# One 512-column product for the rounded input and its residual in both FFNs' up-projections

## The chip, the core and the metric

The kernel runs on one core of a Trainium2 chip. The metric is the device time of one execution in microseconds (us). Engines are called PE (TensorE, matrix products), PEld (its loading of the stationary operand), DVE (VectorE), ACT (ScalarE), POOL (GpSimd) and SP (SyncE, which issues the transfers).

## What is computed

A decoder trunk of two layers on 256 tokens of width 2048. Each layer has a token mixer (forgetting attention in the first, sliding-window attention in the second) and then a gated FFN with a causal convolution of width 3. The change touches the FFN's up-projection, the first line here:

```python
def conv_ffn(h, w_up, conv_w, conv_b, w_down):
    u = h @ w_up                                   # (256, 2048) @ (2048, 11264)
    up = jnp.pad(u, ((0, 0), (CONV_WIDTH - 1, 0), (0, 0)))
    u = sum(up[:, j:j + S] * conv_w[j] for j in range(CONV_WIDTH)) + conv_b
    g, val = u[..., :D_FF], u[..., D_FF:]
    return (jax.nn.silu(g) * val) @ w_down         # D_FF = 5632
...
x = layer_norm(DEEPNORM_ALPHA * x + (1.0 + g2) * conv_ffn(x * (1 + sc2) + sh2, ...))
```

The vectors shift, scale and gate of all sub-layers come from `silu(c) @ ada_w[i] + ada_b[i]`, which is a product of one row with 2048 x 12288 weights for each layer.

## The kernel before, in words

**Three products for one.** Every large product is made of operands that are split in two: the value rounded to the matrix format (`h`, here `hH`; `wh`) and the residual (`hL`; `wl`). The product is then hH·wh + hL·wh + hH·wl, summed in one PSUM bank. A weight tile `w` holds 2 x 128 rows and 512 columns (512 KB). ACT rounds it to `wh` (line 266) and DVE subtracts to get `wl` (line 277); `wh` and `wl` have four buffers each (pool `hl`), `w` has ten.

**The up-projection.** `w_stationary` (line 328) makes one block of 512 columns of `u`, transposed: the weights are the stationary operand, and hH or hL, stored as 16 tiles of 128 x 256 (features x tokens), moves. `w_mm` (line 311) handles one weight tile: for each of its two row halves `i` and for each of four 128-column blocks `f` it issues three products of 256 columns, so 24 for a tile, 192 for a block of 512 columns (8 tiles). Four blocks share two PSUM banks, two in each, 256 columns wide. An FFN has 22 such blocks, 11 for the gate half and 11 for the value half, in turns, so both FFNs have 44 of them, 352 tiles and 8448 products. They run in two stages for each FFN (12 and 10 blocks), each followed by its part of the down-projection, in which `gT` (the gated result) is stationary and 512 columns of weights move.

**The evacuation.** After a block, `evac` (line 1063) is put into a list that is advanced one step at every weight tile (`run_post`, line 249). For each of the four blocks `f`, `conv` (line 1054) reads PSUM three times: ACT scales and adds the bias (line 1056, into the tile `u`), and two DVE operations add the shifted taps (lines 1057, 1059). The gate half then goes through Silu on ACT (line 1075). The value half is multiplied on DVE (line 1080) and split into `gT` by ACT and DVE (lines 84, 85). Two `yield`s per block spread the four blocks over eight weight tiles.

**Work in the background.** While the FFN runs, DVE also accumulates the ada products (line 395, `acc`), so many steps for each weight tile as a rate says (0.64 in the first FFN, 0.4 in the second), and at the start of each FFN the layer norm's affine part (lines 657 and 658, 24 pairs of 128 x 512 in the trace over three uses).

**What sets the order.** The kernel is written as a list of steps, and the framework's scheduler orders the instructions of each engine from it when the program is built; each engine then runs its list strictly in order. PSUM is one pool of eight banks, shared by products, transposes and the rest. At the start of an FFN the input is made in pieces: `modulate` (line 506) normalises and transposes 128-column pieces of x (line 484), and `mod_pair` (line 488) writes hH and hL.

Of the kernel before, what the change touches and what calls it, by code (L numbers as in the profile page):

```python
# [17 lines left out]
P = 128  # L18
D = 2048
S = 256  # L20
# [21 lines left out]
def hybrid_trunk(ctx: ExitStack, tc: tile.TileContext, a: dict, out: bass.AP):  # L42
# [25 lines left out]
    def w_banks():  # L68
        return [bank("ws").rearrange("p (a s) -> p a s", a=2) for _ in range(2)]
# [4 lines left out]
    def mm(o, lhsT, rhs, start=False, stop=False, **kw):  # L74
        return nc.tensor.matmul(o, lhsT, rhs, start=start, stop=stop, **kw)  # L75
# [11 lines left out]
    def split_v(h, l, src):  # L87
# [13 lines left out]
    nc.gpsimd.memset(ident, 0.0)  # L101
    nc.gpsimd.affine_select(out=ident, in_=ident, compare_op=ALU.not_equal, fill=1.0, base=0,
                            pattern=[[-1, P]], channel_multiplier=1)
    onep = cst.tile([P, P], F32, name="onep")
    nc.gpsimd.memset(onep, 1.0 / P)

    mask = cst.tile([P, 3, P], F32, name="mask")
    nc.gpsimd.memset(mask, 0.0)
# [10 lines left out]
                                    fill=1.0, base=-b, pattern=[[-1, FH]], channel_multiplier=1)  # L119

    x = cst.tile([P, NT, D], F32, name="x")
    csil = cst.tile([KC, P], F32, name="csil")
    nc.scalar.activation(csil, rows0[:KC, 0, :], AF.Silu)
    cact = cst.tile([P, KC], F32, name="cact")
    pt = bank()
# [47 lines left out]
    def rotary():  # L173

        nc.gpsimd.dma_start(sink, a["swa_sinks"][0].partition_broadcast(P))
        posr = cst.tile([NT, P], I32, name="posr")
# [3 lines left out]
        posf = cst.tile([NT, P], F32, name="posf")  # L180
        nc.vector.tensor_copy(posf, posr)
        yield
        pt = bank()
# [127 lines left out]
    def w_mm(ps, kc, h, l, last=KC - 1, first=0):  # L311

        for i in range(2):
            for f in range(4):
# [56 lines left out]
    def ada_vector(l, v):  # L371
# [26 lines left out]
        if row:  # L398
            while not ada["gate_free"]:
                yield  # L400
            ada["gate_free"] = False
            g = cst.tile([P, D], F32, tag="gate", name="gate")
            for j in range(D // 512):
                ps = bank()
                mm(ps, onep, acc[:, j * 512:(j + 1) * 512], start=True, stop=True)
                yield
                nc.scalar.activation(g[:, j * 512:(j + 1) * 512], ps, AF.Copy, bias=1.0)
            gates[l, v] = g
            return
        ps = []  # L410
# [638 lines left out]
    def conv_ffn(l):  # L1049
# [2 lines left out]
        cw = lambda j, f: ccol[:, l, j, f:f + 1]  # L1052

        def conv(pf, f):
            u = tp.tile([P, S], F32, tag="u", bufs=3, name="u")
            nc.scalar.activation(u, pf, AF.Identity, bias=cw(CW, f), scale=cw(2, f))  # L1056
            nc.vector.scalar_tensor_tensor(u[:, 1:], pf[:, :S - 1], cw(1, f), u[:, 1:],  # L1057
                                           op0=ALU.mult, op1=ALU.add)
            nc.vector.scalar_tensor_tensor(u[:, 2:], pf[:, :S - 2], cw(0, f), u[:, 2:],  # L1059
                                           op0=ALU.mult, op1=ALU.add)  # L1060
# [12 lines left out]
        def silu(sil):  # L1073
# [95 lines left out]
```

## Time and profile before

| | us |
|---|---|
| time, median of 3 runs (2255.63 to 2259.47) | 2257.53 |
| span of the profiled execution, first to last instruction | 2251.9 |
| PE busy | 2197.1 (98%) |
| PEld busy | 2017.8 (90%) |
| DVE busy | 1794.3 (80%) |
| ACT busy | 1175.0 (52%) |
| first FFN, up stages | 473 to 751 and 883 to 1107 |
| second FFN, up stages | 1498 to 1772 and 1905 to 2129 |

The page gives no time of its own for the profiled execution beside the span. The median of the runs is 5.6 us above that span: this is what lies around the first and the last instruction, and the prediction adds it to a span. In the rows of the trace, "a<-b,c" is the tile written and the tiles read; the first number of a row of the timeline is the start in us from the span's start, the second its length. Rows of one engine may overlap: an instruction's length holds a tail in which the next one already runs.

### The profile page before, as it was taken

Reading aid. Unit: us, or ns where it says so; the run is one execution under the profiler, and the core shown is the slowest. Engines: PE = TensorE matmul, PEld = TensorE weight load, DVE = VectorE, ACT = ScalarE, POOL = GpSimd, SP = SyncE. Lnnn points to the kernel's source line nnn. Section 1 sums busy time; section 2 is a strip of 40 time slices with the busy share of each in tenths; the row PEclk is TensorE's granted clock in tenths of the full one; section 3 lists DMA queues with packets and bytes.
Section 4 is the critical chain, followed back from the end, with each engine's and each line's share of the span. In section 5 each row is a group of like instructions: output and inputs, shape, how many; then the busy total and the mean of one; then the engine's idle time right before and its main releaser. Section 6 shows DMA issues by size and latency. Waiting matters only on the chain. (4 is left out here: it accounts for less than half of the span.)

```text
span 2251.9 us, 38292 instructions
## 1 busy us (share of the span) xinstructions
PE 2197.1 (98%) x14853; PEld 2017.8 (90%) x14853; DVE 1794.3 (80%) x2450; ACT 1175.0 (52%) x1897; POOL 22.8 (1%) x53
## 2 busy tenths in 40 slices
PE   6999999999999999999999999999999999999997
PEld 6999888889999888999987788889999888999986
DVE  6989999979978968788788989779787555666756
ACT  3445656555555443655634588755555533454532
POOL 0000000000000000000000000000000000000000
PEclk9999999999999999999999999999999999999999
DMA  9999999969979989789897767658887566666663
GB/s 339 381 360 365 361 345 323 329 202 339 324 240 310 322 285 337 249 302 309 265 313 282 256 231 251 215 162 303 264 265 257 177 193 194 188 188 189 190 193 112
DMA packets 274248, 602.99 MB, mean 268 GB/s; under 512 B 21063, under 2 KB 29961, under 8 KB 273553
## 3 DMA queue, kind: packets, MB, share of 16 engines
q1 hardware_dynamic: 273008, 595.85, 79.3%
q0 software_dynamic: 1056, 4.69, 0.6%
q8 instruction: 116, 1.90, 0.3%
q14 instruction: 68, 0.55, 0.1%
HBM read 598.37 MB, written 2.10 MB: 267 GB/s over the span
## 5 line engine op out<-in xcount | busy, mean ns | idle before, releaser
L266 ACT CAST wh<-w 128x1024 fp32r<-128x1024 f32 x728 | 764.1, 1051 | 836.0 <-PE ws L75 304.6
L277 DVE TENSOR_TENSOR wl<-w,wh 128x1024 fp32r<-128x1024 f32 x728 | 888.1, 1223 | 352.6 <-ACT wh L266 331.8
L75 PE MATMUL ws<-hH,wh 128*128 128x256 f32 x3328 | 935.2, 282 | 4.9 <-ACT hH L84 2.1
L75 PE MATMUL ws<-hH,wl 128*128 128x256 f32 x3328 | 929.7, 281 | 3.2 <-DVE wl L277 3.1
L75 PE MATMUL ws<-hL,wh 128*128 128x256 f32 x3328 | 931.2, 280 | 0.0
L75 PEld LDWEIGHTS ws<-hH,wh 128*128 128x128 f32 x3328 | 628.7, 189 | 9.4 <-ACT hH L84 2.3
L75 PEld LDWEIGHTS ws<-hL,wh 128*128 128x128 f32 x3328 | 629.9, 189 | 2.9 <-issue 1.9
L75 PEld LDWEIGHTS ws<-hH,wl 128*128 128x128 f32 x3328 | 628.0, 189 | 4.7 <-DVE wl L277 4.6
L75 PE MATMUL xs<-wh,gT 128*128 128x512 f32 x1408 | 435.9, 390 | 0.0
L75 PEld LDWEIGHTS xs<-wh,gT 128*128 128x128 f32 x1408 | 264.4, 188 | 54.8
L75 PE MATMUL xs<-wl,gT 128*128 128x512 f32 x704 | 274.1, 389 | 0.0
L395 DVE SCALAR_TENSOR_TENSOR acc<-wa,cact,acc 128x1024 f32<-128x1024 f32 x180 | 228.5, 1277 | 0.3 <-DMA wa<-in_ada_w_dram 0.3
L395 DVE SCALAR_TENSOR_TENSOR acc<-wa,cactp,acc 128x1024 f32<-128x1024 f32 x128 | 162.7, 1279 | 1.0 <-DMA acc<-in_ada_b_dram 1.0
L75 PEld LDWEIGHTS xs<-wl,gT 128*128 128x128 f32 x704 | 132.2, 188 | 27.0
L75 PE MATMUL xs<-wl,hH 128*128 128x512 f32 x352 | 141.0, 401 | 3.1 <-DVE wl L277 3.1
L75 PE MATMUL xs<-wh,hH 128*128 128x512 f32 x352 | 142.0, 409 | 0.3 <-ACT hH L494 0.3
L75 PE MATMUL xs<-wh,hL 128*128 128x512 f32 x352 | 138.7, 397 | 0.0
L1056 ACT ACTIVATE u<-ws,ccol 128x256 f32<-128x256 f32 x176 | 96.5, 561 | 57.6 <-PE ws L75 49.1
L75 PE MATMUL xs<-wh,oT 128*128 128x512 f32 x384 | 125.1, 395 | 0.1
L1057 DVE SCALAR_TENSOR_TENSOR u<-ws,ccol,u 128x255 f32<-128x255 f32 x176 | 82.9, 480 | 19.0 <-ACT u L1056 19.0
L75 PEld LDWEIGHTS xs<-wh,oT 128*128 128x128 f32 x384 | 72.1, 188 | 14.8 <-ACT oT L84 0.5
L1059 DVE SCALAR_TENSOR_TENSOR u<-ws,ccol,u 128x254 f32<-128x254 f32 x176 | 83.6, 480 | 2.1
(218 smaller groups left out, 1597.3 us busy)
## 6 DMA issues: line engine op xcount, KB each, us to landing
w<-in_ffn_w_up_dram SPq DMA_DIRECT2D x352, 512.0 KB, 4.6
wa<-in_ada_w_dram SPq DMA_DIRECT2D x320, 512.0 KB, 5.5
w<-in_ffn_w_down_dram SPq DMA_DIRECT2D x176, 512.0 KB, 5.0
w<-in_fox_w_in_dram SPq DMA_DIRECT2D x96, 512.0 KB, 7.2
wo<-in_ada_w_dram SPq DMA_DIRECT2D x48, 512.0 KB, 8.9
w<-in_swa_w_in_dram SPq DMA_DIRECT2D x40, 512.0 KB, 5.3
w<-in_fox_w_o_dram SPq DMA_DIRECT2D x32, 512.0 KB, 6.0
w<-in_swa_w_o_dram SPq DMA_DIRECT2D x32, 512.0 KB, 5.2
```

The source lines that it names most:

```text
L75: return nc.tensor.matmul(o, lhsT, rhs, start=start, stop=stop, **kw)
L266: pin(nc.scalar.copy(h, w), False)
L277: pin(nc.vector.tensor_tensor(l, w, f32(h), op=ALU.subtract), behind[0] > 0)
L395: pin(nc.vector.scalar_tensor_tensor(ac, wo, (cactp if row else cact)[:, k:k + 1], ac, op0=ALU.mult, op1=ALU.add), True)
L1056: nc.scalar.activation(u, pf, AF.Identity, bias=cw(CW, f), scale=cw(2, f))
L1057: nc.vector.scalar_tensor_tensor(u[:, 1:], pf[:, :S - 1], cw(1, f), u[:, 1:], op0=ALU.mult, op1=ALU.add)
L1059: nc.vector.scalar_tensor_tensor(u[:, 2:], pf[:, :S - 2], cw(0, f), u[:, 2:], op0=ALU.mult, op1=ALU.add)
```

## The change

hH and hL become the two halves of one tile, `hHL` (16 x 2 x 256), so that a piece of hH and the piece of hL lie side by side. A new `u_mm` issues, for each stationary block, one product of wh with 512 columns (hH and hL at once) and one of wl with the 256 columns of hH. The 512 columns fill a bank: its left half collects hH·wh + hH·wl, its right half hL·wh. So each of the four blocks gets a bank of its own (four banks for a block of 512 columns instead of two), and the loops are turned: `f` is the outer loop, the row half `i` the inner. In `conv` ACT copies the right half to SBUF (tile `c`), and DVE adds it to the left half in place in PSUM, before the three old operations. One of the two `yield`s for each block goes. The SBUF that `c` takes comes from three small tiles, which move into the ring of tile `t`, and from the constant `onep`, which goes (its factor 1/128 becomes a scale of the ACT operation behind it).

```diff
-    onep = cst.tile([P, P], F32, name="onep")
-    nc.gpsimd.memset(onep, 1.0 / P)
...
-    csil = cst.tile([KC, P], F32, name="csil")
+    csil = tp.tile([KC, P], F32, tag="t", name="csil")
...
+    def u_banks():
+        return [bank("us").rearrange("p (a s) -> p a s", a=2) for _ in range(4)]
+
+    def u_mm(ps, kc, h, l):
+
+        for f in range(4):
+            for i in range(2):
+                wh, wl = h[:, i, f * P:(f + 1) * P], l[:, i, f * P:(f + 1) * P]
+                mm(ps[f], wh, hHL[:, kc + i], start=kc + i == 0, skip_group_check=True)
+                mm(ps[f][:, 0, :], wl, hH[:, kc + i, :], stop=kc + i == KC - 1, skip_group_check=True)
...
     def w_stationary(wsrc, col):
-        ps = w_banks()
-        stream(wsrc, 0, col, list(range(KC)), lambda kc, h, l: w_mm(ps, kc, h, l))
+        ps = u_banks()
+        stream(wsrc, 0, col, list(range(KC)), lambda kc, h, l: u_mm(ps, kc, h, l))
...
-                mm(ps, onep, acc[:, j * 512:(j + 1) * 512], start=True, stop=True)
+                mm(ps, ones, acc[:, j * 512:(j + 1) * 512], start=True, stop=True)
...
-    hH = cst.tile([P, KC, S], F32R, name="hH")
-    hL = cst.tile([P, KC, S], F32R, name="hL")
+    hHL = cst.tile([P, KC, 2, S], F32R, name="hHL")
+    hH, hL = hHL[:, :, 0, :], hHL[:, :, 1, :]
...
         def conv(pf, f):
+            c = tp.tile([P, S], F32, tag="c", bufs=2, name="c")
+            nc.scalar.copy(c, pf[:, 1, :])
+            pf = pf[:, 0, :]
+            nc.vector.tensor_tensor(pf, pf, c, op=ALU.add)
             u = tp.tile([P, S], F32, tag="u", bufs=3, name="u")
...
             for f in range(5):
-                v = conv(ps[f // 2][:, f % 2, :], f0 + f) if f < 4 else None
+                v = conv(ps[f], f0 + f) if f < 4 else None
                 if u is not None:
                     then(f - 1, u)
                 u = v
                 yield
-                yield
```

The forgetting attention's own projections keep `w_mm` and its 256-column products. Three places show how the engines' lists move.

PE, in the middle of a weight tile of the first FFN's first block, before (two stationary blocks, three products each):

```order
L75 MATMUL ws<-hH,wh 128x256
L75 MATMUL ws<-hL,wh 128x256
L75 MATMUL ws<-hH,wl 128x256
L75 MATMUL ws<-hH,wh 128x256
L75 MATMUL ws<-hL,wh 128x256
L75 MATMUL ws<-hH,wl 128x256
```

and now, the same place (`us` are the new banks), where two stationary blocks take four products:

```order
L75 MATMUL us<-hHL,wh 128x512
L75 MATMUL us<-hHL,wl 128x256
L75 MATMUL us<-hHL,wh 128x512
L75 MATMUL us<-hHL,wl 128x256
L75 MATMUL us<-hHL,wh 128x512
```

Each pair of 256-column products with the same `wh` has become one of 512, and one load of `wh` has gone with it.

PE at the start of the first FFN, before (`sm<-ident,x` are the transposes of x; in brackets the engine whose signal is waited for):

```order
L484 MATMUL sm<-ident,x 128x128 [waits Activation_49]
L484 MATMUL sm<-ident,x 128x128 x3
L484 MATMUL sm<-ident,x 128x128 [waits DVE_49]
L484 MATMUL sm<-ident,x 128x128 x3
L75 MATMUL ws<-hH,wh 128x256 [waits Activation_49]
L75 MATMUL ws<-hH,wh 128x256
L484 MATMUL sm<-ident,x 128x128
L484 MATMUL sm<-ident,x 128x128 [waits DVE_49]
L484 MATMUL sm<-ident,x 128x128 x2
L484 MATMUL sm<-ident,x 128x128 [waits DVE_49]
```

and now:

```order
L493 MATMUL sm<-ident,x 128x128 [waits Activation_49]
L493 MATMUL sm<-ident,x 128x128 x3
L493 MATMUL sm<-ident,x 128x128 [waits DVE_49]
L493 MATMUL sm<-ident,x 128x128 x3
L75 MATMUL us<-hHL,wh 128x512 [waits DVE_49,Activation_49]
L75 MATMUL us<-hHL,wl 128x256
L75 MATMUL us<-hHL,wh 128x512 [waits DVE_49,Activation_49]
```

The first product now waits for DVE's hL as well, and eight transposes that stood between the first products stand behind the first weight tile.

DVE, in the evacuation of the first FFN's second block (a value half), before:

```order
L277 TENSOR_TENSOR wl<-w,wh 128x1024 [waits DMAHW1_49,PE_49]
L1057 SCALAR_TENSOR_TENSOR u<-ws,ccol,u 128x255
L1080 TENSOR_TENSOR u<-u,sil 128x256 [waits DVE_49]
L1059 SCALAR_TENSOR_TENSOR u<-ws,ccol,u 128x254 [waits DVE_49]
L277 TENSOR_TENSOR wl<-w,wh 128x1024 [waits DMAHW2_49,PE_49,Activation_49]
L85 TENSOR_TENSOR gT<-u,gT 128x256 [waits Activation_49]
L395 SCALAR_TENSOR_TENSOR acc<-wa,cactp,acc 128x1024 [waits DMAHW3_49]
L277 TENSOR_TENSOR wl<-w,wh 128x1024 [waits DMAHW4_49,PE_49]
```

and now, where the same block's evacuation begins:

```order
L1067 TENSOR_TENSOR us<-us,c 128x256 [waits Activation_49]
L275 TENSOR_TENSOR wl<-w,wh 128x1024 [waits DMAHW4_49,PE_49,Activation_49]
L1070 SCALAR_TENSOR_TENSOR u<-us,ccol,u 128x255 [waits Activation_49]
L1067 TENSOR_TENSOR us<-us,c 128x256
L1072 SCALAR_TENSOR_TENSOR u<-us,ccol,u 128x254 [waits DVE_49]
L404 SCALAR_TENSOR_TENSOR acc<-wa,cactp,acc 128x1024 [waits DMAHW3_49]
L1070 SCALAR_TENSOR_TENSOR u<-us,ccol,u 128x255 [waits Activation_49]
L1092 TENSOR_TENSOR u<-u,sil 128x256 [waits DVE_49]
L1072 SCALAR_TENSOR_TENSOR u<-us,ccol,u 128x254 [waits DVE_49]
L275 TENSOR_TENSOR wl<-w,wh 128x1024 [waits DMAHW5_49,PE_49]
```

Between two subtractions `wl` there stand seven other operations now where there were three, since a block is evacuated at every tile and not at every second one, and each brings an addition more.

More of the change, by code (lines that the diff above doesn't have):

```diff
@@ L175, in rotary @@
         nc.gpsimd.dma_start(sink, a["swa_sinks"][0].partition_broadcast(P))
-        posr = cst.tile([NT, P], I32, name="posr")
+        posr = tp.tile([NT, P], I32, tag="t", name="posr")
         nc.gpsimd.dma_start(posr, a["positions"].rearrange("b (t p) -> (b t) p", p=P))
@@ L179, in rotary @@
         nc.vector.tensor_scalar_mul(nsink, sink, -1.0)
-        posf = cst.tile([NT, P], F32, name="posf")
+        posf = tp.tile([NT, P], F32, tag="t", name="posf")
         nc.vector.tensor_copy(posf, posr)
@@ L404, in ada_vector @@
                 ps = bank()
-                mm(ps, onep, acc[:, j * 512:(j + 1) * 512], start=True, stop=True)
+                mm(ps, ones, acc[:, j * 512:(j + 1) * 512], start=True, stop=True)
                 yield
-                nc.scalar.activation(g[:, j * 512:(j + 1) * 512], ps, AF.Copy, bias=1.0)
+                nc.scalar.activation(g[:, j * 512:(j + 1) * 512], ps, AF.Copy, bias=1.0, scale=1.0 / P)
             gates[l, v] = g
```

## The prediction

> **What bounds the kernel now.** I read the page's first part, then the busy time by stretches of one block of 512 columns (22.4 us), and then the timeline of PE inside a stage.
>
> ```profile
> PE 2197.1 (98%) x14853; PEld 2017.8 (90%) x14853; DVE 1794.3 (80%) x2450; ACT 1175.0 (52%) x1897; POOL 22.8 (1%) x53
> ```
>
> PE is never idle for long. That alone does not say that PE is the bound in the stage that changes, so here are the stretches, four of the first FFN's first stage, two of its second, two of the second FFN's first stage and two of its last. The columns are the stretch, its length, then busy time and instructions of PE, PEld, DVE, ACT and POOL, granted clock, DMA share and GB/s.
>
> ```profile
> 505.40:527.80 22.40, 22.09 (x190) 21.88 (x189) 22.40 (x30) 12.39 (x16) 0.00 (x0) 1.00 0.93 308
> 527.80:550.20 22.40, 22.40 (x195) 22.40 (x194) 22.40 (x31) 11.96 (x16) 0.00 (x0) 1.00 0.99 365
> 550.20:572.60 22.40, 22.40 (x195) 22.40 (x194) 21.86 (x27) 12.73 (x18) 0.00 (x0) 1.00 0.99 355
> 572.60:595.00 22.40, 22.40 (x195) 22.40 (x194) 22.07 (x32) 12.07 (x17) 0.00 (x0) 1.00 0.94 323
> 1017.50:1039.90 22.40, 22.40 (x194) 22.40 (x193) 21.33 (x29) 11.93 (x17) 0.00 (x0) 1.00 0.89 290
> 1039.90:1062.30 22.40, 22.40 (x194) 22.40 (x193) 18.82 (x21) 11.76 (x17) 0.00 (x0) 1.00 0.93 325
> 1524.40:1546.80 22.40, 22.40 (x194) 22.40 (x194) 22.36 (x32) 12.77 (x17) 0.00 (x0) 1.00 0.88 296
> 1546.80:1569.20 22.40, 22.40 (x194) 22.40 (x194) 21.47 (x31) 12.12 (x18) 0.00 (x0) 1.00 0.95 332
> 2014.00:2036.40 22.40, 22.40 (x194) 22.40 (x194) 13.22 (x16) 11.68 (x16) 0.00 (x0) 1.00 0.65 187
> 2036.40:2058.80 22.40, 22.40 (x194) 22.40 (x194) 15.75 (x24) 11.85 (x16) 0.00 (x0) 1.00 0.68 190
> ```
>
> PE works through all of them, at full granted clock. DVE has a third of its time free in the last stage, some 10% in the first FFN's second stage, and nothing at the start of the first FFN. How far ahead of PE DVE is decides what more work on it costs:
>
> ```profile
> 522.19 1.23 DVE L277 TENSOR_TENSOR wl<-w,wh 128x1024 fp32r<-128x1024 f32 x1
> 523.48 0.39 PE L75 MATMUL ws<-hH,wl 128*128 128x256 f32 x1 [0.31 <-DVE wl L277]
> 2003.18 1.05 ACT L266 CAST wh<-w 128x1024 fp32r<-128x1024 f32 x1 [0.95 <-PE ws L75]
> 2007.06 1.23 DVE L277 TENSOR_TENSOR wl<-w,wh 128x1024 fp32r<-128x1024 f32 x1 [1.24 <-ACT wh L266]
> ```
>
> In the last stage DVE waits for ACT and ACT waits for PE to free one of four buffers: both are as far ahead as the buffers allow. At 523.48 the opposite holds: PE waits 0.31 us for a `wl` that ended at 523.42. So **PE is the bound in 43 of the 44 blocks, and DVE in the one around 520 us**.
>
> **The change, part by part.** First the products. Their pitch (start to start) decides, not their length, since they overlap.
>
> ```profile
> 2000.06 0.28 PE L75 MATMUL ws<-hL,wh 128*128 128x256 f32 x1
> 2011.96 0.28 PE L75 MATMUL ws<-hL,wh 128*128 128x256 f32 x1
> ...
> 1799.92 0.39 PE L75 MATMUL xs<-wl,gT 128*128 128x512 f32 x1
> 1811.48 0.39 PE L75 MATMUL xs<-wl,gT 128*128 128x512 f32 x1
> ...
> 1254.63 0.40 PE L75 MATMUL xs<-wh,hH 128*128 128x512 f32 x1
> 1257.43 0.40 PE L75 MATMUL xs<-wh,hH 128*128 128x512 f32 x1
> ```
>
> Between the first two rows lie 102 products of 256 columns: 11.90 / 102 = 116.7 ns each. Between the next two lie 51 of 512 columns in the down-projection: 11.56 / 51 = 226.7 ns. The last two, with 12 products between them, are of 512 columns as well, with hH as the stationary operand: 2.80 / 12 = 233.3 ns. The trace has no product with 512 columns of hH and hL moving. Its bounds are these two rows: at 233.3 it costs just what two products of 256 cost, and the gain is nothing; at 226.7 it saves 6.67 ns. No row of 512 columns is slower than two of 256, so a loss on PE is excluded as far as rows go. I take 226.7, since the stationary operand of the new product is a small streamed buffer, as gT is, and hH is not loaded. There are 8448 / 3 = 2816 such pairs: 2816 x 6.67 = **18.8 us less**. A further gain could lie in the product of `wl` that follows, whose load now hides behind 512 columns:
>
> ```profile
> 1100.47 0.60 PE L433 MATMUL sm<-ident,acc 128*128 128x128 f32 x4
> L433 PE MATMUL sm<-ident,acc 128*128 128x128 f32 x96 | 14.0, 274 | 1.4 <-DVE acc L395 1.4
> ```
>
> Transposes of 128 columns come at (0.60 - 0.274) / 3 = 109 ns, which no product with a load of its own undercuts here. If 256 columns came down to that, 2816 x (116.7 - 109) = 22 us more would go. I take none: the load of the next `wh` still has to hide behind those 256 columns, as now.
>
> Here the Trainium skill can be weighed, "TensorE: Matmul & The Clock Gate", section "Back-to-back issue gap": a warm product takes its columns over 2.4 GHz and 2.5 ns on top. By that only 2.5 ns go with each merged pair, an estimate of 2816 x 2.5 = 7.0 us in place of 18.8. The rows disagree with it in size (116.7 for 256 columns, where it gives 109), so I keep the rows.
>
> Second, the additions. Each of the 176 blocks of 128 columns gets one more DVE operation of 256 columns and one ACT copy.
>
> ```profile
> L616 DVE TENSOR_TENSOR x<-x,t 128x512 f32<-128x512 f32 x48 | 32.8, 684 | 0.2
> L614 DVE TENSOR_TENSOR t<-xs,gate 128x512 f32<-128x512 f32 x48 | 31.6, 684 | 12.5 <-PE xs L75 12.4
> 1999.98 0.42 DVE L85 TENSOR_TENSOR gT<-u,gT 128x256 fp32r<-128x256 f32 x1
> 2000.32 0.48 DVE L1059 SCALAR_TENSOR_TENSOR u<-ws,ccol,u 128x254 f32<-128x254 f32 x1
> 2000.71 0.42 DVE L85 TENSOR_TENSOR gT<-u,gT 128x256 fp32r<-128x256 f32 x1
> ```
>
> An operand in PSUM costs DVE nothing extra at 512 columns (684 ns both). The addition is new in writing PSUM. It cannot cost less than nothing, being added work; from above the tap operation bounds it, pitch 0.39; the plain 256-column operation has pitch 0.34, and I take that: 4 x 0.34 = 1.36 us more DVE per 512 columns. PE needs 22.4 - 64 x 0.00667 = 21.97 us for these now. The ACT copy is bounded by two rows:
>
> ```profile
> L712 ACT COPY pT<-T 128x384 f32<-128x384 f32 x48 | 22.7, 473 | 0.4
> L84 ACT CAST oT<-o 64x256 fp32r<-64x256 f32 x24 | 8.7, 363 | 4.8 <-PE o L75 4.4
> ```
>
> Four of them at 0.36 to 0.47 bring ACT from 12 to about 13.7 of 21.97 us: hidden by ACT's idle time. If ACT were full, 176 x 0.36 = 63 us would show.
>
> What the additions cost is read stage by stage. In the last stage DVE goes to 17.1 of 21.97: nothing. In the first FFN's second stage a value and a gate block take 21.33 + 18.82 + 2.72 = 42.9 of 43.9: nothing, with `wl` tiles waiting in four buffers to cover a value block's 22.7. In the first FFN's first stage the first three stretches quoted come to 22.40 + 22.40 + 21.86 + 4.08 = 70.7 us against 65.9 of PE, with no stock left at 523: 4.8 us too much, of which a part was DVE working ahead (it catches up by 570); I take **4 us**, at least 2, and with no stock at all some 4 more in later value blocks. In the second FFN two stretches come to 46.6 against 43.9, but PE has no wait for `wl` there now, so some stock is left: **1 us**. Evacuating a block at every tile instead of every second one brings this work earlier in the block and is in these numbers.
>
> Third, the start of each FFN.
>
> ```profile
> 473.01 0.54 PE L75 MATMUL ws<-hH,wh 128*128 128x256 f32 x2 [0.33 <-ACT hH L494]
> 473.35 1.91 PE L484 MATMUL sm<-ident,x 128*128 128x128 f32 x8
> 474.16 0.75 DVE L496 TENSOR_TENSOR hL<-t,hH 128x256 fp32r<-128x256 f32 x2
> 474.91 0.56 PE L75 MATMUL ws<-hL,wh 128*128 128x256 f32 x1
> ...
> 1500.05 0.56 PE L75 MATMUL ws<-hL,wh 128*128 128x256 f32 x1
> ```
>
> Now the first product needs both hL pieces (DVE, done at 474.91), and the eight transposes that PE did from 473.35 stand behind the first tile. PE is idle from 473.0 to 474.6 or a little later, **1.6 us**, and twice that for two FFNs: 3.2 us, bounded by half of it and, if the granted clock stays low longer, by 5 us each. DVE and ACT are ahead in this time, which is part of why I take 4 and not 4.8 above. The other edits (the layout of hHL, the scale in place of `onep`, the tiles in the ring of `t`) add no instruction; POOL loses one and SP's issues stay in number: nothing.
>
> **The sum** is -18.8 + 4 + 1 + 3.2 = -10.6 us on a span of 2251.9, so 2241.3. The medians of the runs lie 5.6 above the span: **2246.9 us**.
>
> **The rivals.** *512 columns cost what two times 256 cost.* Every pair with hH in it has the same rate in this trace, 233.3 for 512 and 116.7 for 256, and only gT and oT do better. Then nothing is gained and the 8.2 us stay: 2257.5 + 8.2 = **2265.7**, slower. It decides from a pitch of 226.7 + 6.67 - 8.2 / 2.816 = 230.4 ns upward. For it speaks that equality; against it that hH was loaded in that row and is streamed in the new one.
>
> *DVE becomes the bound in the first FFN.* The chain of a block now goes PE, ACT copy, DVE addition, ACT, DVE, DVE, and both engines run in order; an ACT queue that stands before a DVE addition stands before the next `wh` too. With half a microsecond of such gaps in each of 22 blocks DVE needs 22.0 on average and the first FFN loses its 9.4 us of gain: 2246.9 + 9.4 = **2256.3**, no change. Against it speaks the stock of `wl` in all blocks but the early ones.
>
> *Something in between:* a pitch of 230, the middle of both rows, gains 9.4 us, and the time is again **2256.3**. The skill's 2.5 ns per pair are near this, 2257.5 - 7.0 + 8.2 = 2258.7, an estimate.
>
> *The load hides better:* 256 columns at 109 ns too, 2246.9 - 22 = **2225**.
>
> **How the numbers follow.** The forecast has a chance of 0.40, equal cost 0.28, DVE as the bound 0.14, in between 0.10, the better load 0.08. A measurement of this kernel tells 0.2% (4.5 us) from no change. Of the forecast's 0.40, 0.35 are faster, 0.03 same, 0.02 slower (its costs could be 15 us instead of 8.2); of equal cost 0.25 slower and 0.03 same; of DVE as the bound 0.02, 0.05, 0.07; of in between 0.02, 0.04, 0.04; the better load is faster. Together faster 0.47, same 0.15, slower 0.38. The range from 2230 to 2268 leaves out most of the last case and the worst 0.1 of the slower ones; both signs being near, the likeliest case's own range is 2241 to 2254.
>
> **What would show it.** Right or wrong is read first from the pitch of two `us<-hHL,wh` rows with a `us<-hHL,wl` between: 343 ns for the forecast, 350 for the rival, in the last stage, where DVE is idle. Then from the last stage's length: 10 blocks in 219.7 us instead of 224. The cost shows as PE waiting for `wl` between 500 and 600 us, and as idle PE before the first `us` row. DVE's addition should have a pitch near 0.34. The prediction is wrong if PE waits for `wl` in the second stages, if the pitch is 350, or if ACT's `wh` waits for DVE's additions.

## The result, and the profile after

The changed kernel takes **2255.54 us** (median of 12 runs, 2253.07 to 2258.84), the kernel before 2257.41 in runs beside it (12 runs, 2255.23 to 2261.49). The ratio is 0.999, with a 95% interval from 0.9981 to 0.9998: 0.5 to 4.3 us less, where the forecast was 10.6 us less: about a fifth of it. The profiled execution has a span of 2254.8 us and a time of its own of 2256.56.

First the pitch, in the last stage. The two rows of 512 columns below have 32 other such rows between them, and a `wl` product behind each:

```profile
2000.08 0.39 PE L75 MATMUL us<-hHL,wh 128*128 128x512 f32 x1
2000.30 0.28 PE L75 MATMUL us<-hHL,wl 128*128 128x256 f32 x1
2000.42 0.39 PE L75 MATMUL us<-hHL,wh 128*128 128x512 f32 x1
...
2011.52 0.39 PE L75 MATMUL us<-hHL,wh 128*128 128x512 f32 x1
```

33 pairs take 11.44 us: **346.7 ns each**, where the triple before took 350.0 and the forecast was 343.3. Inside a pair the 512 columns take 228.5 ns and the 256 columns 118.2 (means of over 2700 steps each). The gain is 350.0 - 346.67 = 3.33 ns a pair: 2816 x 3.33 = 9.4 us.

Then the starts of the two FFNs, the first with the rows ahead of it:

```profile
473.07 1.12 PE L493 MATMUL sm<-ident,x 128*128 128x128 f32 x4 [2.43 <-ACT x L646]
...
474.58 1.11 PE L493 MATMUL sm<-ident,x 128*128 128x128 f32 x4 [0.40 <-DVE x L648]
...
476.72 0.75 DVE L505 TENSOR_TENSOR hHL<-t,hHL 128x256 fp32r<-128x256 f32 x2
...
477.28 0.77 PE L75 MATMUL us<-hHL,wh 128*128 128x512 f32 x1 [1.58 <-DVE hHL L505]
...
1504.72 0.76 PE L75 MATMUL us<-hHL,wh 128*128 128x512 f32 x1 [1.58 <-DVE hHL L505]
```

PE waits 1.58 us for DVE's hL, twice, as forecast. What the forecast left at nothing can be seen in the granted clock. These are stretches of 24 us around both starts, of the kernel before:

```profile
466.00:490.00 24.00, 20.39 (x149) 19.16 (x149) 21.27 (x38) 15.06 (x22) 1.12 (x2) 0.93 0.41 115
1490.00:1514.00 24.00, 20.48 (x147) 19.02 (x146) 21.27 (x37) 15.15 (x22) 1.11 (x2) 0.93 0.36 112
```

and of the changed kernel:

```profile
466.00:490.00 24.00, 19.59 (x91) 16.12 (x90) 18.18 (x33) 12.04 (x18) 1.12 (x2) 0.79 0.31 104
1490.00:1514.00 24.00, 19.60 (x85) 15.86 (x85) 16.83 (x30) 11.58 (x16) 1.11 (x2) 0.79 0.26 93
```

The clock (the column ahead of the DMA share) falls from 0.93 to 0.79. At half clock (stretches of 1 us from 474 and from 481 us show 0.50) that is 0.07 x 24 / 0.5 = 3.4 us before and 10.1 us after. The Trainium skill, "TensorE: Matmul & The Clock Gate", section "What's actually happening", has the clock decided in windows of about 3.4 us; the stretches here (3.4, 6.7 and 10.1 in the runs below) are steps of that size.

That the wait lengthens the half clock is not shown, though. The kernel before, profiled once more, and the version without the additions (a run below), whose PE waits for hL as the changed kernel's does, lie closer together:

```profile
466.00:490.00 24.00, 20.39 (x121) 17.92 (x120) 18.02 (x33) 13.31 (x19) 1.12 (x2) 0.93 0.29 100
1490.00:1514.00 24.00, 21.16 (x105) 17.87 (x104) 16.73 (x30) 12.39 (x17) 1.11 (x2) 0.86 0.31 99
```

```profile
466.00:490.00 24.00, 19.14 (x95) 15.86 (x94) 18.59 (x33) 12.74 (x19) 1.12 (x2) 0.86 0.33 109
1490.00:1514.00 24.00, 18.69 (x95) 15.60 (x94) 18.96 (x34) 12.68 (x19) 1.11 (x2) 0.86 0.33 107
```

Nor does the mean clock of the executions follow the wait: it is 0.9888 for the kernel before and 0.9889 with the start mended, neither of which has the wait, and 0.9894 without the additions, which has it.

Third, DVE in the early first FFN, and what the additions are. The first fence holds PE's waits between 476 and 756 us, the next a row of the timeline, the third groups of the page:

```profile
PE us L75 <- DVE wl L275: 3.2, 3, 1.6
PE us L75 <- DVE hHL L505: 1.6, 1, 1.6
```

```profile
523.96 1.22 DVE L275 TENSOR_TENSOR wl<-w,wh 128x1024 fp32r<-128x1024 f32 x1
...
525.23 0.38 PE L75 MATMUL us<-hHL,wl 128*128 128x256 f32 x1 [1.64 <-DVE wl L275]
```

```profile
L1067 DVE TENSOR_TENSOR us<-us,c 128x256 f32<-128x256 f32 x176 | 71.1, 424 | 0.0
L1065 ACT COPY c<-us 128x256 f32<-128x256 f32 x176 | 61.6, 372 | 9.5 <-PE us L75 7.3
L1069 ACT ACTIVATE u<-us,ccol 128x256 f32<-128x256 f32 x176 | 98.1, 562 | 39.4 <-DVE us L1067 39.4
```

PE waits three times for `wl`, 3.2 us together against 0.3 us before. After 570 us there is no such wait in either FFN. ACT does wait 39.4 us for the additions, but that is idle time of an engine that is no bound.

Stage by stage, in us from the first product of one stage to the first of the next (the start is from the last product of the projection ahead):

| stage | before | after | start mended | no addition | two of 256 | mixed | slower early ada |
|---|---|---|---|---|---|---|---|
| up to the first FFN | 467.7 | 470.2 | 472.6 | 470.6 | 469.9 | 468.7 | 469.4 |
| start, first FFN | 5.3 | 7.0 | 5.5 | 7.0 | 5.5 | 5.5 | 5.5 |
| first FFN, first up stage | 277.5 | 279.6 | 277.8 | 276.1 | 281.3 | 277.0 | 275.6 |
| first FFN, second up stage | 227.0 | 224.9 | 224.9 | 224.9 | 227.0 | 224.9 | 224.9 |
| start, second FFN | 5.3 | 7.0 | 5.5 | 7.0 | 5.3 | 5.3 | 5.5 |
| second FFN, first up stage | 276.6 | 275.3 | 274.9 | 275.0 | 276.5 | 274.5 | 275.2 |
| second FFN, last up stage | 224.0 | 221.9 | 221.9 | 221.9 | 224.0 | 221.9 | 221.9 |

The second stages gain 2.1 us, which is 640 x 3.33 ns. The starts lose 1.7 each. The first up stages should have gained 2.6 us each (12 blocks): the second FFN's gains 1.3, the first FFN's loses 2.0. The first line differs by 2.5 us, though hardly anything was changed there; a run below takes that up. (In the kernel before the second and third up stage end at 1110 and 1775 us, not at the 1107 and 1772 given above.)

### The profile page after: what moved, and what is told of

It is laid out like the page before. It is cut to its first block, busy times and chain, and to the rows that moved or that the text cites. A ratio compares the mean times of both kernels' runs of the same rounds, so it can differ in the third digit from the quotient of the medians.

```text
span 2254.8 us, 33096 instructions
## 1 busy us (share of the span) xinstructions
PE 2196.5 (97%) x12037; PEld 1901.8 (84%) x12037; DVE 1847.4 (82%) x2626; ACT 1220.7 (54%) x2073; POOL 22.6 (1%) x52
## 5 line engine op out<-in xcount | busy, mean ns | idle before, releaser
L75 PE MATMUL us<-hHL,wh 128*128 128x512 f32 x2816 | 985.7, 393 | 3.2 <-DVE hHL L505 3.2
L75 PE MATMUL us<-hHL,wl 128*128 128x256 f32 x2816 | 792.0, 283 | 3.2 <-DVE wl L275 3.2
L75 PEld LDWEIGHTS us<-hHL,wh 128*128 128x128 f32 x2816 | 530.2, 188 | 115.8 <-ACT hHL L503 3.9
L75 PEld LDWEIGHTS us<-hHL,wl 128*128 128x128 f32 x2816 | 534.4, 190 | 8.0 <-DVE wl L275 4.6
L75 PE MATMUL xs<-wh,hHL 128*128 128x512 f32 x704 | 238.5, 404 | 0.3 <-ACT wh L264 0.2
L75 PE MATMUL ws<-hHL,wh 128*128 128x256 f32 x1024 | 190.1, 288 | 4.4 <-ACT hHL L84 2.1
L75 PEld LDWEIGHTS ws<-hHL,wh 128*128 128x128 f32 x1024 | 162.0, 195 | 7.4 <-ACT hHL L84 2.7
L75 PEld LDWEIGHTS xs<-wh,hHL 128*128 128x128 f32 x704 | 131.8, 190 | 30.0 <-issue 1.0
L75 PE MATMUL ws<-hHL,wl 128*128 128x256 f32 x512 | 143.7, 288 | 2.2 <-DVE wl L275 2.2
L75 PE MATMUL xs<-wl,hHL 128*128 128x512 f32 x352 | 141.7, 403 | 1.5 <-DVE wl L275 1.4
L1069 ACT ACTIVATE u<-us,ccol 128x256 f32<-128x256 f32 x176 | 98.1, 562 | 39.4 <-DVE us L1067 39.4
```

## The experiments

Times are put as ratios to the kernel before, in runs on the same chip (medians there 2258.2 to 2260.0 us); the changed kernel itself stands at 0.999. The 95% intervals reach some 0.001 to either side, so a difference of 2 or 3 us between two versions lies at the edge of the noise, and the stages of the table must bear it out.

**The start mended.**

```diff
+        if kc < nfirst[0]:
+            for i in range(2):
+                for f in range(4):
...
+                    mm(ps[f][:, 0, :], wh, hH[:, kc + i, :], start=kc + i == 0, skip_group_check=True)
+                    mm(ps[f][:, 0, :], wl, hH[:, kc + i, :], skip_group_check=True)
+            for i in range(2):
+                for f in range(4):
+                    mm(ps[f][:, 1, :], h[:, i, f * P:(f + 1) * P], hL[:, kc + i, :], skip_group_check=True)
+            return
```

> The first weight tile of each FFN is done in 256-column products, the 16 that need only hH first and the 8 with hL last; all else is the changed kernel (2255.5 us). Theory A (the product pair is 346.7 ns and not 343.3, gain 9.4 us, and the starts and the early stall of DVE give it back): PE's wait of 2.0 us before the first product goes, the half-clock stretch of 10.2 us at each FFN's start falls back to 3.4, and the time falls by 2 to 3 us for the second FFN and by 0 to 3 for the first, where DVE becomes late next: about 2251. Rival B (the starts lie beside DVE's backlog and cost nothing; the gain is lost in the additions alone): 2255.5, and the waits for wl near 520 us grow by what the start gives.

0.9978 (0.9969 to 0.9987), 2253.39 us: 2.7 us below the changed kernel by the ratios. PE goes from the transposes straight into the products, and the clock of the same stretch is 0.86:

```profile
476.94 1.11 PE L505 MATMUL sm<-ident,x 128*128 128x128 f32 x4 [0.39 <-DVE x L660]
478.07 0.58 PE L75 MATMUL us<-hHL,wh 128*128 128x256 f32 x1
```

```profile
466.00:490.00 24.00, 20.94 (x108) 17.49 (x107) 17.94 (x33) 13.07 (x19) 1.12 (x2) 0.86 0.33 107
```

Theory A holds in size, at the low end of its 2 to 6 us: the two rows of the starts give back 1.5 us each. Rival B falls: the waits for `wl` did not grow but fell to 1.7 us. The half clock did not fall to 3.4 us as expected; it stays at 6.7 us, as long as in the version without the additions, which still has the wait.

**No addition.**

```diff
-            c = tp.tile([P, S], F32, tag="c", bufs=2, name="c")
-            nc.scalar.copy(c, pf[:, 1, :])
             pf = pf[:, 0, :]
-            nc.vector.tensor_tensor(pf, pf, c, op=ALU.add)
```

> The changed kernel without ACT's copy and DVE's addition: the right half of each bank is computed and never read, so the contribution of hL times wh is left out of the result. Theory A: only the early first FFN was short of DVE time, so the gaps before wl products at 523, 530 and 553 us (4.2 us together) go and the time falls by 4 to 5 us, to about 2251; the product pair stays at 346.7 ns. Rival B (the additions cost all of the missing gain, by writing PSUM while PE accumulates there): the pair falls to 343 ns and the time by 10 us or more, to 2245 or less.

0.9975 (0.9964 to 0.9985), 2252.69 us: 3.4 below the changed kernel. The first FFN's first stage takes 276.1 in place of 279.6; every other stage is within 0.4 of the changed kernel, and the pair stays at 346.7. So ACT's copies and DVE's additions cost 3.4 us, all in that stage. Rival B falls with the pair.

**Two of 256.**

```diff
-                mm(ps[f], wh, hHL[:, kc + i], start=kc + i == 0, skip_group_check=True)
+                mm(ps[f][:, 0, :], wh, hH[:, kc + i, :], start=kc + i == 0, skip_group_check=True)
+                mm(ps[f][:, 1, :], wh, hL[:, kc + i, :], skip_group_check=True)
```

> The changed kernel with each 512-column product made as two of 256 columns into the two halves of the same bank; banks, loop order, copy and addition stay. Theory A: the triple is 350.0 ns against 346.7, so the last stage takes 223.9 us instead of 221.8 and the time rises by 9.4 us, to about 2265. Rival of equal cost (the 512-column product gains nothing and the shorter stages come from the order of the loops or the banks): no change, 2255.5. Forecast as predicted (18.8 us in the products, lost elsewhere): 2274.

1.0014 (1.0005 to 1.0023), 2261.85 us: 5.4 above the changed kernel, not 9.4. The stages say why: the products cost their 9.4 us again (the two second stages are back at 227.0 and 224.0), but the first product waits for hH alone again, so both starts fell back to 5.5 and 5.3, 3.2 us together. The expectation had left that out. The last stage is 224.0 as before: banks and loop order do nothing to the pitch.

**The second `yield` restored** in `evac`.

> The changed kernel with the second yield of each evacuation step restored, so that a block's additions are spread over eight weight tiles again and its four banks stay in use longer. Theory A: the early first FFN lacks DVE time in sum, not in order, so 2255.5 within 1.5 us, and the gaps before wl products only move. Rival C (the bunched evacuation is what holds up the wl subtractions): the gaps at 523 to 554 us shrink below 1 us together and the time falls by 3 to 4 us. Rival D: banks are freed too late, PE waits for a bank at the start of a block, some us slower.

0.9991 (0.998 to 1.0001), 2256.03 us: as theory A has it, no change. PE's waits for `wl` become one of 1.8 us in place of three of 3.2 us together; the stage is 279.1.

**Mixed.** The first six blocks of the first FFN and the first two of the second are made the old way.

```diff
+                old = b < (3, 1)[l]
-                ps = w_stationary(w_up, b * WB)
+                ps = w_stationary(w_up, b * WB, old)
```

> The first six blocks of the first FFN and the first two of the second are made as in the kernel before (256-column products, two banks, two yields, no copy, no addition); the other 36 blocks as in the changed kernel. Theory A (the stages' difference to the kernel before is made of 0.21 us gained in every block, 1.7 us and about 1.2 us of half clock lost at each start, and about 3.6 us lost to DVE before 570 us): both losses go, 36 x 0.21 = 7.6 us stay, so 7 to 8 us below the kernel before and about 5.5 below the changed kernel; no PE wait for wl over 0.5 us anywhere in the FFNs. Rival B (the additions cost time in every block): the first FFN's second stage and the second FFN's stages are not shorter than in the changed kernel, and the whole gains less than 4 us on the kernel before.

0.9962 (0.995 to 0.9975), 2249.63 us: 8.6 us below the kernel before, a little over the 7 to 8 expected. PE's wait for `wl` is 0.3 us, as before. With both losses gone the gain of the products is what remains, so rival B (a cost in every block) falls.

**Slower early ada**, on top of the mended start.

```diff
             for b in range(b0, b1):
+                if l == 0 and si == 0:
+                    then(lambda b=b: ada.update(rate=0.4 if b < 2 else 0.76))
```

> The changed kernel with the first weight tile of each FFN done in 256-column products as in the run on the start, and with the ada accumulation slowed in the first four blocks of the first FFN (0.4 steps for each weight tile in place of 0.64) and made up in the other eight blocks of that stage (0.76). All 44 blocks but the first tiles keep the 512-column product and the additions. Theory A (early DVE is short by the sum of its work, and has room later): the gaps before wl products near 523 to 553 us shrink to under 1 us together, the first FFN's first stage takes about 275 us (277.8 in the run on the start), and the whole is 7 to 9 us below the kernel before, equal to the mixed kernel within a microsecond or two. Rival E (DVE has no room later either): the waits come back between 570 and 750 us and the stage stays at 277 us or more.

0.9959 (0.9945 to 0.9972), 2248.49 us: the fastest version, 9.3 us below the kernel before. PE waits for no `wl` in the first FFN's first stage, which takes 275.6 us, 2.1 less than with the mended start alone. DVE's early shortage was the sum of its work in some 100 us, and the additions fit in once other work makes room.

Those six runs settle the bookkeeping. The rest asks why the pair takes 346.7 ns and not 343.3.

**Grouped:** the eight products of 512 columns of a tile first, then the eight of 256.

```diff
         for f in range(4):
             for i in range(2):
-                mm(ps[f], wh, hHL[:, kc + i], start=kc + i == 0, skip_group_check=True)
-                mm(ps[f][:, 0, :], wl, hH[:, kc + i, :], stop=kc + i == KC - 1, skip_group_check=True)
+                mm(ps[f], h[:, i, f * P:(f + 1) * P], hHL[:, kc + i], start=kc + i == 0, skip_group_check=True)
+        for f in range(4):
+            for i in range(2):
+                mm(ps[f][:, 0, :], l[:, i, f * P:(f + 1) * P], hH[:, kc + i, :], stop=kc + i == KC - 1,
+                   skip_group_check=True)
```

> The changed kernel with the products of a weight tile in another order: the eight of 512 columns first, then the eight of 256. Theory P (a change of length between two products in a row costs time, since the next load hides behind a shorter product): 14 of 16 steps are between equals, 512 columns come at 226.7 ns and 256 at 116.7, the pair at 343.5 in the mean, the last stage at about 219.9 us instead of 221.8, and the whole some 8 us faster than the changed kernel. Theory Q (512 columns of hH and hL moving cost 228.5 and 256 of hH behind a load of wl cost 118.2, whatever stands beside): 346.7 and no change in the last stage. The wl products come later in a tile, so the early waits for wl may shrink by about 1 us in both cases.

1.003 (1.0018 to 1.0042), 2266.16 us. Neither theory had this. Rows of the last stage, eight products in the second and in the third:

```profile
2001.62 2.03 PE L75 MATMUL us<-hHL,wh 128*128 128x512 f32 x8
2003.48 1.11 PE L75 MATMUL us<-hHL,wl 128*128 128x256 f32 x8
2004.42 0.86 PE L75 MATMUL us<-hHL,wh 128*128 128x512 f32 x3
```

1.86 / 8 = 232.5 and 0.94 / 8 = 117.5 ns: the equal cost of the prediction's first rival, and the last stage takes 224.5 us. The mixture of lengths does not cost the missing half. In this layout it is what brings the gain.

**All of 512 columns.**

```diff
-                mm(ps[f][:, 0, :], wl, hH[:, kc + i, :], stop=kc + i == KC - 1, skip_group_check=True)
+                mm(ps[f], wl, hHL[:, kc + i], stop=kc + i == KC - 1, skip_group_check=True)
```

> The product of wl takes 512 columns too (hH and hL moving), which adds the term hL times wl to the result; every product of the up-projection then has 512 columns. Theory P (the mix of lengths costs): all at 226.7 ns as in the down-projection, 453.3 for two, the last stage of ten blocks at 640 x 0.4533 = 290.1 us. Theory Q (it is the moving tile): about 228.5 each, 457 for two, 292.5 us. Rival H (hH as an operand of 512 columns costs what it costs as stationary operand in the attention projections): 233.3 each, 298.7 us.

2589.24 us. Rival H holds: the rows below are 20 products apart, 4.67 / 20 = 233.5 ns, and the last stage takes 298.7 us.

```profile
2000.23 0.39 PE L75 MATMUL us<-hHL,wh 128*128 128x512 f32 x1
...
2004.90 0.39 PE L75 MATMUL us<-hHL,wh 128*128 128x512 f32 x1
```

**Zeros** in hH and hL (`nc.vector.memset(G, 0.0)` and the same for `B`, ahead of `modulate`).

> The changed kernel with scale and shift of the inputs of the sliding-window projections and of both FFNs set to zero, so that hH, hL and all that is made of them hold zeros; instructions, shapes and places stay, two small DVE operations more at each start. Theory Z (the pitch depends on the values that go through PE): 512 columns with hH stationary in the attention projections fall from 233.3 to about 226.7 ns, and the pair in the FFN from 346.7 to 343 or less (the last stage to 219.7 us or less). Theory Y (it does not): 233.3, 346.7 and 221.8 us again.

2255.89 us. Two rows with 33 pairs between them:

```profile
2020.23 0.39 PE L75 MATMUL us<-hHL,wh 128*128 128x512 f32 x1
...
2031.67 0.39 PE L75 MATMUL us<-hHL,wh 128*128 128x512 f32 x1
```

11.44 / 33 = 346.7 ns again, and 233.1 in the attention projections: theory Y. The values of hH and hL play no part.

**Shifted by 32 bytes:** a small tile ahead of hHL moves it and all that lies behind it.

> A tile of 32 bytes is placed ahead of hHL, so that hHL begins at 32 modulo 64 bytes in SBUF and the weights, wh, wl and gT at 0, the other way round than in the changed kernel. Theory S (the place of the operands in a 64-byte row sets the pitch): 512 columns of hHL fall to 226.7 ns and the down-projection's products, with wh and wl moving, rise from 226.7 to 228 or more. Theory Q (it does not): 228.5 and 118.2 in the up-projection, 226.7 in the down-projection, as before.

2253.03 us. All pitches as in the changed kernel, so theory S falls. hHL and the weights stay 32 bytes apart modulo 128 here, so the shift moved them together. What it left untried was their distance.

**Another place for gT.**

```diff
+    gp = ctx.enter_context(tc.tile_pool(name="gp", bufs=30))
     cst = ctx.enter_context(tc.tile_pool(name="cst", bufs=1))
...
-    gp = ctx.enter_context(tc.tile_pool(name="gp", bufs=30))
```

> The changed kernel with the pool of gT and oT placed first in SBUF, so that gT lies at the low addresses (10 to 72 KB of each partition) and hHL, wh and wl higher (89 to 122 KB and 181 KB up); the program is otherwise the same. Theory S2 (the place in SBUF of what PE reads sets 233.3 against 226.7): the down-projection's 512-column products leave 226.7 ns, or those of the attention projections leave 233.3. Theories Z and Y: all pitches as in the changed kernel, 226.7, 233.3 and 228.5 with 118.2.

2271.16 us: the down-projection, which the change doesn't touch, leaves its 226.7 ns. 48 products lie between these rows of its third stage, 11.20 / 48 = 233.3:

```profile
1822.34 0.39 PE L75 MATMUL xs<-wl,gT 128*128 128x512 f32 x1
...
1833.54 0.39 PE L75 MATMUL xs<-wl,gT 128*128 128x512 f32 x1
```

So the place in SBUF of the operands changes the pitch. gT began at 96 modulo 128 bytes, as wh and wl do, and begins at 0 here; hH, which gave 233.3 as stationary operand in the prediction's rows, begins at 0 with the weights at 96. The next runs move hHL against the weights.

**hHL and the weights at the same place** (a tile of 32 bytes behind hHL, so all begin at 0 modulo 128), in the changed kernel, in the kernel before, and in the fastest version.

```diff
     hHL = cst.tile([P, KC, 2, S], F32R, name="hHL")
+    shift = cst.tile([P, 8], F32, name="shift")
```

> The changed kernel with a tile of 32 bytes behind hHL, so that hHL, the weights, wh, wl and gT all begin at 0 modulo 64 bytes (hHL at 0 and the others at 32 in the changed kernel). Theory S3 (products whose moving and stationary operand differ by 32 bytes modulo 64 are slower by a thirty-fifth): 512 columns of hHL at 226.7 ns and 256 at 113 to 117, the pair at 340 to 343.4, the last stage at 217.6 to 219.8 us instead of 221.8; the attention projections with hH stationary fall from 233 to 226.7; together 12 to 30 us below the changed kernel. Theory T (what moves gT matters by its distance, not by its place modulo 64): no change, 2255.5 and 346.7.

> The kernel before with a tile of 32 bytes behind hL, so that hH, hL, the weights, wh and wl all begin at 0 modulo 64 bytes. Theory S3: products of 256 columns fall from 116.7 to about 113.3 ns, a triple to 340, the last stage of ten blocks from 224.2 to about 218 us; 8448 x 3.3 = 28 us in the FFNs and some 5 us in the projections, less where DVE is late: 2225 to 2235. Theory S3 with a floor by the load of the stationary operand (256 columns cannot come faster than 116.7): only the projections gain, 2252 or so. Theory T: no change.

> The version with mended starts and slower early ada accumulation, with hHL and the weights at the same place modulo 64 bytes. Theory S3: what the changed kernel gains by the same step comes on top of 2248.5, so 2219 to 2237, unless DVE, with less than 21.9 us for a block, becomes late in the first FFN. Theory T: 2248.5.

1.0019 (1.0007 to 1.003), 1.0099 (1.0086 to 1.0113) and 0.9995 (0.9986 to 1.0004): theory S3 falls, since all three are slower than without the shift, and so does theory T, since the place does count. In the last stage of the changed kernel with the shift, 33 pairs between the first two rows and, in the attention projections, 15 steps between the last two, each the first of two products in a row:

```profile
2020.24 0.40 PE L75 MATMUL us<-hHL,wh 128*128 128x512 f32 x1
...
2031.90 0.40 PE L75 MATMUL us<-hHL,wh 128*128 128x512 f32 x1
```

```profile
1258.21 0.63 PE L75 MATMUL xs<-wh,hHL 128*128 128x512 f32 x2
...
1261.62 0.62 PE L75 MATMUL xs<-wh,hHL 128*128 128x512 f32 x2
```

and in the last stage of the kernel before with the shift, 96 products between:

```profile
2030.31 0.28 PE L75 MATMUL ws<-hL,wh 128*128 128x256 f32 x1
...
2041.83 0.28 PE L75 MATMUL ws<-hL,wh 128*128 128x256 f32 x1
```

The pair rises to 11.66 / 33 = 353.3 ns and the 256-column product of the kernel before to 11.52 / 96 = 120.0, while in the attention projections, with hH stationary, 512 columns fall from 233.3 to about 227 (3.41 / 15 = 227.3). The same distance serves one order of operands and harms the other. It also alters what merging is worth: 3 x 120.0 - 353.3 = 6.7 ns a pair, and between the two kernels with the shift 2282.45 - 2263.06 = 19.4 us, though neither is faster than the kernel before.

**The two other distances.** hHL is allocated ahead of three small tiles and begins at 64 modulo 128; the weights at 0 (with the small tile) or at 96 (without it, in the fastest version).

> As the first of these runs, but hHL is allocated ahead of three small tiles and begins at 64 modulo 128 bytes, the weights, wh, wl and gT at 0 modulo 128. Theory S3 by 64 bytes: the same pitches as in the first run. Theory S3 by 128 bytes or more: 233.3 in the attention projections and 346.7 for the pair.

> The version with mended starts and slower early ada accumulation (2248.5 us), with hHL allocated ahead of three small tiles, so that it begins at 64 modulo 128 bytes and wh, wl and gT at 96 (in the version itself hHL begins at 0): a distance of 96 in place of 32. If only being 32 bytes off a multiple of 64 counts (distances 32 and 96 alike), the pair is 346.7 ns and the time 2248.5 again. If each of the four distances has its own pitch, the pair is anything from 340 to 352; at 343.3 the last stage takes 219.7 us and the time is about 2239.

2264.34 us, and 0.9995 (0.9982 to 1.0008). Two rows with 33 pairs between, of a distance of 64 bytes and then of 96:

```profile
2020.25 0.39 PE L75 MATMUL us<-hHL,wh 128*128 128x512 f32 x1
...
2031.76 0.39 PE L75 MATMUL us<-hHL,wh 128*128 128x512 f32 x1
```

```profile
2020.14 0.39 PE L75 MATMUL us<-hHL,wh 128*128 128x512 f32 x1
...
2031.69 0.39 PE L75 MATMUL us<-hHL,wh 128*128 128x512 f32 x1
```

The last stage does not speak for the others. Around 600 us, in the first FFN's first stage, 33 pairs lie between two rows of a distance of 0 and then of 64:

```profile
600.01 0.39 PE L75 MATMUL us<-hHL,wh 128*128 128x512 f32 x1
...
611.45 0.39 PE L75 MATMUL us<-hHL,wh 128*128 128x512 f32 x1
```

```profile
600.10 0.40 PE L75 MATMUL us<-hHL,wh 128*128 128x512 f32 x1
...
611.76 0.40 PE L75 MATMUL us<-hHL,wh 128*128 128x512 f32 x1
```

These are 11.44 / 33 = 346.7 and 11.66 / 33 = 353.3 ns: at these two places the pair has more than one pitch in one run. The four distances side by side:

| hHL less weights, modulo 128 bytes | pair around 600 us, ns | pair in the last stage, ns | last stage, us |
|---|---|---|---|
| 0 | 346.7 | 353.3 | 226.1 |
| 32 (the changed kernel; also both moved by 32) | 346.7 | 346.7 | 221.9 |
| 64 | 353.3 | 348.9 | 223.3 |
| 96 | 350.0 | 350.0 | 224.0 |

So 346.7 is the least that any of the four shows, and at 32 bytes it holds in all four up stages, by the luck of the layout. No order, no values and no place tried here gave 343.3. That 0 differs from 64, and 32 from 96, excludes a period of 64 bytes; that the period is 128 is assumed, since no run moved a tile by 128 bytes alone.

**The kernel before once more.**

> The kernel before once more, for a second profile. Its first profile reached the end of the forgetting attention's output projection at 467.7 us, the nine profiles with the change at 468.2 to 474.9. Theory N (that part is the same work and scatters from run to run): this profile lies between 468 and 475 as well, and the half-clock stretches differ from those of the first profile. Theory O (the moved small tiles and the new layout of hH cost 2 to 3 us there): 467 to 468 again.

2262.98 us; it reached the first FFN at 474.5 us, 6.8 later than in its first profile. Theory N: the 2.5 us of the table's first line are scatter of that part, and the half clock at the second FFN's start, shown above, scatters too. So does the pitch. Between these rows lie 33 triples, of this profile and then of the first:

```profile
579.85 0.28 PE L75 MATMUL ws<-hL,wh 128*128 128x256 f32 x1
...
591.51 0.28 PE L75 MATMUL ws<-hL,wh 128*128 128x256 f32 x1
```

```profile
579.93 0.28 PE L75 MATMUL ws<-hL,wh 128*128 128x256 f32 x1
...
591.48 0.28 PE L75 MATMUL ws<-hL,wh 128*128 128x256 f32 x1
```

The same program, with all tiles at the same places, takes 11.66 / 33 = 353.3 ns a triple here and 11.55 / 33 = 350.0 there. The slower pitch ends at 640 us, and the first FFN's first stage takes 278.6 us in place of 277.5. The run with two of 256 has it too, up to 648 us, in its stage of 281.3.

## Why the prediction was wrong

- **The products: the step that failed.** "I take 226.7, since the stationary operand of the new product is a small streamed buffer, as gT is, and hH is not loaded" gave 343.3 ns a pair and 18.8 us. Measured are 346.7 and 9.4 us: the mechanism was right and its size was off by half. Being streamed was not what set gT's rows apart from hH's: with gT moved in SBUF they took 233.3 as well. What the merge saves is no constant to be borrowed: it was 3.3 ns here, nothing with the products grouped, and 6.7 in the last stage with the tile shifted. The 256-column product was taken as unchanged at 116.7 and costs 118.2. The rival "in between" had the right gain (9.4), by taking a middle, not by knowing why. The Trainium skill, "TensorE: Matmul & The Clock Gate", section "Back-to-back issue gap", gave 2.5 ns a pair, an estimate of 7.0 us; it gives that figure for a product by itself and says that in a stream the loads count as well. With 3.3 ns measured its size was nearer than the row that was preferred to it, but by luck: a fixed cost of each product would have stayed with the products grouped, where the pair takes 350.0.
- **The better load** did not come: 118.2 ns for 256 columns, not 109. Nor is 109 the floor that the text reads it as: in the kernel before, the product `S<-Bm,A` of 128 columns, which has a load of its own, starts at 286.52 us and the next product at 286.58.
- **The additions**, forecast at 4 + 1 us: 3.4 + 0. The pitch was forecast at 0.34 us, and the last stage's rows show it (two additions with one operation of the same size between them):

```profile
2004.80 0.43 DVE L1067 TENSOR_TENSOR us<-us,c 128x256 f32<-128x256 f32 x1
2005.13 0.41 DVE L1092 TENSOR_TENSOR u<-u,sil 128x256 f32<-128x256 f32 x1
2005.47 0.43 DVE L1067 TENSOR_TENSOR us<-us,c 128x256 f32<-128x256 f32 x1
```

- **The starts**, forecast at 3.2: 3.4 as idle time. The text named the clock as a bound and put it at nothing. In this profiled execution the two first up stages lose some 2.4 us more beside the longer half clock: 1.3 in the second FFN (276.6 - 2.6 + 1.3 = 275.3) and 1.1 in the first (277.5 - 2.6 + 3.4 + 1.1 = 279.4, where 279.6 is measured). That the clock takes them, and that the wait lengthens it, is not shown. With the start mended the second FFN's stage still takes 274.9, and the kernel before differs from itself by 1.0 us in the first FFN's stage.
- **The sum.** Of the two profiles, costs of 9.2 in place of 8.2 stand against a gain of 9.4 in place of 18.8: 0.2 us of gain, and 2.6 if the 2.4 are scatter. Another 0.5 us lies behind the start of the last product (14.2 us to the end before, 13.7 now), which no step had and no run explains; with two of 256 it is 14.2 again, in the mixed kernel 14.0. The 0.7 to 3.1 together are inside the measured 0.5 to 4.3. The large part of the miss, 9.4 us, is the pitch.
- **The base.** 5.6 us were added to the span for what lies around it. The changed kernel's profiled execution shows 2256.56 - 2254.8 = 1.8; the other 3.8 were this execution of the kernel before being a short one. The forecast difference is not touched by it.

What stays open is what makes the distance count, why 32 bytes are best for the one pair of operands and 0 for the other, and what moves a stream of products from one pitch to another at the same place. Loads run while products run (PEld is busy for 1901.8 us and PE for 2196.5 of the changed kernel's 2254.8), so two operands are read at a time, and the distance, the order and the lengths may all shift the one reading against the other. That is a guess, which no run here tests.

## What to carry to other kernels

Before a pitch is borrowed from another row of a trace, look at where the operands of both lie: the same shape took 226.7 or 233.3 ns by the place of a tile modulo 128 bytes, and a row that differs in two things (streamed or not, and place) doesn't tell which one counts. Measure a pitch in every stage and in a second profile: one stage, or one execution, may show another. A merged instruction that needs two producers waits for the later one; keep the first tile in the old form. Where an addition overloads an engine for one stretch only, thin out other work of that engine in that stretch: 275.6 us against 277.8 for the stage here.

## What was not expected of the hardware

- A shift of an SBUF tile by some tens of bytes changes the pitch of products by up to 3%: 120.0 against 116.7 ns for 256 columns, 233.3 against 226.7 or 227.3 for 512. In the kernel before, 32 bytes of an empty tile cost 22 us (1.0099).
- At one place the pitch can have two values: 346.7 and 353.3 ns for the pair in two stages of one run (distance 0), 350.0 and 353.3 for the triple in two executions of one program.
- At a distance of 32 bytes a product of 512 columns with hH and hL moving costs 233.5 ns among its like and 228.5 with one of 256 between.
